# A dilated mixer whose second and third group read a copy of h in class order, written by GpSimd

## The chip, the cores and the metric

The kernel runs on one core of one Trainium2 chip. The metric is the device time of one execution in microseconds. TensorE multiplies (a load of the stationary operand, then the product with the moving operand, into PSUM), VectorE and ScalarE do the elementwise work, GpSimd is nearly unused, and SP's queue issues the loads from memory.

## The reference

Two transformer blocks in sequence on x, 512 tokens of 1024 features: a first block of two layers (an even mixer, a convolutional feed-forward, a dilated mixer, a second convolutional feed-forward) and a second block with modulated layers. Only the dilated mixer matters here. h is the normalised x.

```
z = (h @ w_in).reshape(B, S, 3, 3, 4, 128)      # groups, (q, k, v), heads, features
q = rmsnorm(z[:, :, :, 0], q_gain)
k = rmsnorm(z[:, :, :, 1], k_gain)
v = z[:, :, :, 2]
for g, (window, dilation) in enumerate(((128, 1), (512, 4), (2048, 16))):
    o_g, lse_g = dilated_branch(q[:, :, g], k[:, :, g], v[:, :, g], dilation, window // dilation)
...
wts = softmax(stack(lses), axis=0)
o = sum(wts[..., None] * stack(outs), axis=0)
return o.reshape(B, S, 512) @ w_out
```

A query t of a group attends to t, t - dilation, t - 2 * dilation and so on. So the tokens of groups two and three fall into classes by t modulo the dilation; the kernel uses 4 classes for both (group three masks the keys whose distance within a class is no multiple of 4).

## The kernel before

Features lie on the partitions and tokens on the free axis. h stands in SBUF as 8 k tiles of 128x512, each as a pair of rounded part and rest (`hh`, `hl`); weights come from memory in blocks of 256 columns, as `raw` tiles of 4 k tiles, and are split in units of 2 k tiles into `whi` (ScalarE) and `wlo` (VectorE). Every product is three products (`mm3`: high by high, and two mixed ones). TensorE's order is the order of the program: `gemm` gives feature-major keys and queries, with the weights stationary and 512 columns of h moving into PSUM tile `gm`; `gemm_tok` gives token-major values, with a slice of 128 tokens of h stationary and 256 columns of weights moving into PSUM tile `gt`. After each k tile `tick` issues further splits and the next stages of tasks: `k_norm` and `q_scale` (PSUM tiles `ss` and `qst`, VectorE factors), then `odd_scores` (PSUM tile `os`; VectorE takes the row maximum, ScalarE the exponential into `pr`). A task is issued when a model of the engines' times says that its inputs are there and that PSUM banks are free. `finish(su)` issues all that is left of a list of tasks. SP's loads go out in the order in which a dry run recorded the weights' use, each when a `raw` buffer (there are 4) is free. All 128x512 work tiles come from one pool of 66.

In the dilated mixer, keys and queries of groups one, two and three come first, in this order, with the scores as tasks between them. For groups two and three the ScalarE copies out of PSUM reorder the columns by class (`cls`, `clsps`). Then come the values:

```
for gi in range(3):
    sls = [slice(t * P, (t + 1) * P) for t in range(4)] if gi == 0 else \
          [slice(r, S, 4) for r in range(4)]
    ...
        for t, p in enumerate(self.gemm_tok(w(gi * 6 + 4 + b), NK, h, sls)):
            nc.scalar.activation(vt[t][:, b * 256:(b + 1) * 256], p, AF.Copy)
```

So group one's slices of h are contiguous, those of groups two and three take every fourth token. `finish(su)` stands ahead of group two's values; behind it the tasks `odd_weights` (PSUM tiles `nat` and `cl`) and `odd_turn` (VectorE scales `pr`, TensorE transposes it into `ot`) run between the remaining values. At the end `odd_out` (PSUM tile `opo`) multiplies values and weights.

Of the kernel before, what the change touches and what calls it, by code (L numbers as in the profile page):

```python
# [19 lines left out]
P = 128  # L20
D = 1024
S = 512
# [55 lines left out]
def bcast(ap, off, n):  # L78
    """a row of n elements for every partition"""
    if isinstance(ap, Blank):  # L80
        return ap
    return bass.AP(tensor=ap.tensor, offset=ap.offset + off, ap=[[0, P], [1, n]])


class Blank:
    """stands for any object while the order of the weights is recorded"""
# [11 lines left out]
class Clock:  # L98
    """estimates when the engines get to the instructions, in us, so that they can be issued in a good order"""
# [5 lines left out]
    @staticmethod  # L105
    def span(ap):
        """the tensor's name, and the columns"""
        pitch = ap.ap[0][0]
        a = ap.offset % pitch if pitch else 0
        return ap.tensor.name, a, a + 1 + sum((n - 1) * abs(st) for st, n in ap.ap[1:])  # L110

    def done(self, ap, engine=None):
        """when the data are there, for an engine"""
        name, a, b = self.span(ap)
        return max([f + (0.1 if e != engine else 0.0 if e == "tensor" else 0.05) for c, d, f, e in self.written.get(name, ()) if c < b and a < d], default=0.0)
# [66 lines left out]
class Kern:  # L182
# [82 lines left out]
    def chore(self, gen):  # L265
        """instructions in stages, each issued when its turn has come"""
        c = [gen, False, (), 0.0]
        self.chores.append(c)
        self.step(c)
# [9 lines left out]
    def unit(self, key, k0, n, w, load, hold=False):  # L279
        """n k tiles of weights, split; unless they are held, those before are done with. load: how many  # L280
        k tiles come from memory together with these, if these are the first of them"""
# [24 lines left out]
    def wahead(self):  # L306
        """a split ahead, if the engines have the time"""
# [32 lines left out]
    def weights(self, key, kt, w=256, first=0):  # L340
        """the weights of k tiles first .. first + kt, a k at a time: (k, hi, lo)"""
        for k0, n, (hi, lo) in self.units(key, kt, w, first):
            for k in range(n):
                yield k0 + k, hi[:, k], lo[:, k]

    def passes(self, srcs, kt, ps, done, first=0, tok=False):
        """several passes over the same weights, which stay on chip meanwhile. ps: list of (h, its columns,
        the psum's columns or None for a psum of its own, a function to call before); done(pass, source,
        psums) comes after each source of a pass."""
# [48 lines left out]
    def gemm(self, src, kt, hs, widths=(128, 128), first=0):  # L398
        """hs: list of (list of (hi, lo) per k, N). Returns psum[m][stream]."""
# [11 lines left out]
    def gemm_m(self, src, kt, h, first=0):  # L411
        """the products of 256 columns, a half of the columns after the other: a single psum at a time"""
# [17 lines left out]
    def gemm_tok(self, src, kt, h, sls):  # L430
        """token-major: for each token slice a psum [128, 256]"""
# [10 lines left out]
    def rsqrt_small(self, v, n, y=None):  # L442
        """1/sqrt(v) for a few columns, on DVE."""
# [12 lines left out]
    def square(self, key, x, k):  # L456
        """the running sum of the chunks' squares; until the last chunks two are side by side"""
# [20 lines left out]
    def stream(self, key):  # L478
        """the chunks of a stream: a half of x, or the context"""
        return self.cs if key == "c" else [x[:, HALF[key]] for x in self.x]  # L480

    def begin_norm(self, key):
        """spawns the norm of a stream whose squares are under way, for the next sublayer"""
# [13 lines left out]
    def norm(self, key, xs, hs, G, Sh):  # L497
        """rmsnorm of 256 tokens over the features (partitions and chunks), of sums of squares that are
        under way -> hs, (hi, lo) of each chunk"""
# [53 lines left out]
    def halves(self, off=True):  # L553
        """the passes over the halves of x"""
# [7 lines left out]
    def mid_steps(self, src, res, n=S):  # L562
        """hi and lo of src, into the list res"""
# [11 lines left out]
    # ---- feed-forward: up pairs -> mids -> partial down products into x  # L575
    def ffn(self, up, down, act, gates, after=None, late=None):
        """gates: by stream, "x" and if need be "c" """
# [48 lines left out]
    def final(self, src, mids, gate, first=0, ctx=None, tables="silu_and_others"):  # L626
        """the last products into x, a half of the tokens after the other, each with the start of its norm"""
# [25 lines left out]
    def done(self, mids):  # L653
        """flushes the chores if a mid is still to be issued in part"""
# [3 lines left out]
    def update(self, x, ps, gate, k):  # L658
        """x += gate * ps"""
# [34 lines left out]
    def proj_out(self, src, gate, mids, first=0):  # L694
        """x += gate * W^T mids, over the k tiles from first on"""
# [11 lines left out]
    def firsts(self, srcs):  # L707
        """the first products of a mixer"""
# [8 lines left out]
    # ---- tasks whose instructions go between the k steps of the large products  # L717
# [5 lines left out]
    def step(self, t):  # L723
        """issues the next stage of a task or chore"""
# [11 lines left out]
    def time(self):  # L736
        """where the tensor engine is"""
# [16 lines left out]
    def start(self, t):  # L754
        """when a task can go on: its inputs are there, and its banks free"""
# [36 lines left out]
    def finish(self, ts):  # L792
        """issues all that is left of the tasks; others only where they hold nothing up"""
# [18 lines left out]
    # ---- modulation vectors, a unit of 256 columns at a time  # L812
# [10 lines left out]
    def mod_task(self):  # L823
# [15 lines left out]
        def sums(i, m, r, u0, n):  # L839
            """the sums over the partitions for n units from u0 on"""  # L840
# [42 lines left out]
    # ---- even mixer of the first block  # L883
# [5 lines left out]
    def even_mixer(self):  # L889
# [27 lines left out]
        # linear attention  # L917
# [26 lines left out]
    def k_norm(self, k, res, i, gain, mat, dh, n, perm=None, post=None):  # L944
        """k <- k * rstd * gain, in place"""
# [11 lines left out]
    def rstd_bc(self, sq, n, mat, cnt):  # L957
        """1/sqrt(mean over mat's blocks of sq + eps), replicated over the block's partitions"""
# [15 lines left out]
    def o_norm(self, o, res, i, gain, extra=None, gate=None):  # L974
        """rmsnorm of a head's output over its 128 features, then hi and lo"""
# [13 lines left out]
    def q_scale(self, ps, res, i, gain, mat, nh, dh, perm=None, post=None, front=False):  # L989
        """q with its gain (unnormalised); a task for the row scales rstd / sqrt(dh), token-major [P, 4 * nh]"""  # L990
# [8 lines left out]
        def task():  # L999
# [5 lines left out]
            # (mean + eps) * dh  ->  rsqrt gives rstd / sqrt(dh)  # L1005
# [20 lines left out]
    def softmax(self, s, cc, p, sm, nb):  # L1026
        """p = exp(cc*(s - max)), sm = row sums; nb = -cc*max"""
# [42 lines left out]
    def log_decay(self, ar, gs):  # L1070
        """log decays, token-major (16 times too large), two tiles of [P, 2 * 256]"""
# [17 lines left out]
    def gla(self, gs):  # L1089
# [37 lines left out]
        # attention inside the chunks  # L1127
# [18 lines left out]
        # states  # L1146
        gs["st"] = st = {}
        for c in range(2):
            prev = None
            sts = [self.g("state") for _ in range(2)]  # L1150
            for n0 in (0, 4):
                ns = [n for n in range(n0, n0 + 4) if n < 7]
                # a bank for each row tile of the array
# [35 lines left out]
    # ---- odd mixer of the first block  # L1189
    def odd_mixer(self):  # L1190
# [3 lines left out]
        H = [(h, S)]  # L1194
# [11 lines left out]
        su = []  # L1206
        for gi in range(3):
            kh = []
            if gi == 0:
                pk = self.firsts([w(2), w(3), w(0)])  # L1210
            for b in range(2):
                for m, ps in enumerate(pk[b] if gi == 0 else [p[0] for p in self.gemm(w(gi * 6 + 2 + b), NK, H)]):
                    k = self.g("ok")
                    if gi == 0:
                        nc.scalar.activation(k, ps, AF.Copy)
                    else:
                        nc.scalar.activation(cls(k), clsps(ps), AF.Copy)
                    kh.append(self.spawn(self.k_norm(k, kt, (gi, 2 * b + m), self.v("od_k_gain"), self.ones, 128, S)))
            for b in range(2):
                for m, ps in enumerate(pk[2] if gi == b == 0 else [p[0] for p in self.gemm(w(gi * 6 + b), NK, H)]):  # L1220
                    hd = 2 * b + m
                    qh = self.q_scale(ps if gi == 0 else clsps(ps), qs, (gi, hd), self.v("od_q_gain"),
                                      self.ones[:, 0:1], 1, 128, perm=None if gi == 0 else cls)
                    prob[gi, hd] = [self.g("pr0"), self.g("pr1")] if gi == 0 else [self.g("pr")]
                    su.append(self.spawn(self.odd_scores(gi, hd, kt, qs, prob[gi, hd], sms, nbs), (kh[hd], qh)))
        # values, in the order of the classes
        val = {}
        co = None
        for gi in range(3):
            sls = [slice(t * P, (t + 1) * P) for t in range(4)] if gi == 0 else \  # L1230
                  [slice(r, S, 4) for r in range(4)]
            vt = [self.g("ov") for _ in range(4)]
            for b in range(2):
                if gi == 1 and b == 0:
                    self.finish(su)
                    gs = {}
                    wg = self.spawn(self.odd_weights(lse, sms, nbs, gs))
                    parts = [[] for _ in range(4)]
                    pts = [self.spawn(self.odd_turn(hd, prob, gs, parts[hd]), [wg]) for hd in range(4)]
                    self.wb = 6  # L1240
                for t, p in enumerate(self.gemm_tok(w(gi * 6 + 4 + b), NK, h, sls)):
                    nc.scalar.activation(vt[t][:, b * 256:(b + 1) * 256], p, AF.Copy)
            val[gi] = vt
# [25 lines left out]
    def odd_weights(self, lse, sms, nbs, gs):  # L1269
        """the rows' factors: weight of the group / row sum, [P, 3, (tile, head)]"""  # L1270
# [58 lines left out]
    def odd_turn(self, hd, prob, gs, res):  # L1329
        """the weights of a head, with the rows' factors, transposed"""  # L1330
# [27 lines left out]
    def odd_out(self, hd, parts, val, res):  # L1358
        """sum over the groups of the weighted values of a head"""
# [17 lines left out]
    # ---- attention mixer of the second block  # L1377
# [75 lines left out]
    def attn_unit(self, t, c, qs, kk, va, ao):  # L1453
        """a pair of heads for 128 tokens; keys of the context, then of x"""
# [39 lines left out]
        # the heads' weighted values, side by side on the array, then over the sums  # L1494
# [12 lines left out]
    def stack_q(self, qs, i, res):  # L1507
        """hi and lo of each head of a pair one below the other"""
# [13 lines left out]
    def stack_k(self, ks, i, res, n):  # L1522
        """by head, hi twice and lo twice"""
# [18 lines left out]
    def pool(self, gi, p0, pw, res):  # L1542
        """(window means - p) @ pool_w: the tokens are mixed last, by a banded matrix"""
# [28 lines left out]
    # ---- gated spatial mixer of the second block  # L1572
# [65 lines left out]
    def mods_of(self, key, norm, row):  # L1638
        """the factors and the shift of a norm: (G(k), Sh(k))"""
# [25 lines left out]
    def context(self):  # L1665
        """loads the context and begins its first norm"""
# [63 lines left out]
def lay_out(inputs):  # L1730
    """Layouts of the inputs, and constants of the shapes."""
# [3 lines left out]
    def blocks(w, cols=None):  # L1735
        """[K, M] -> [M/256, 128, K/128, 256]"""
# [5 lines left out]
    def pm(v):  # L1742
        """[.., n*128] -> [128, .. n]"""
# [69 lines left out]
    # by window: the blocks for the first, the inner and the last tokens, then the columns that a neighbour adds to  # L1813
# [34 lines left out]
```

## Time and profile before

| | us |
|---|---|
| three runs | 3411.66, 3412.04, 3418.02 |
| median | 3412.04 |
| span of the profiled execution, first to last instruction | 3414.8 |
| TensorE busy / weight loads busy | 3366.9 / 2939.6 |
| VectorE busy / ScalarE busy / GpSimd busy | 2098.8 / 1252.8 / 5.0 |

The runs are device times. The profiled execution has no time of its own beside its span, which lies inside the three runs. Weight loads overlap products, so the two rows of TensorE are not to be added. All start times below are microseconds from the start of the span; the dilated mixer lies between about 682 and 1010.

### The profile page before, as it was taken

How to read it: one execution, taken by the hardware profiler on the slowest of the kernel's cores; microseconds unless marked ns; L12 is line 12 of the kernel's file. 1: busy time of each engine (PE TensorE's matmuls, PEld its weight loads, DVE VectorE, ACT ScalarE, POOL GpSimd, SP SyncE). 2: the span in 40 equal slices, each digit the busy share in tenths (PEclk: the TensorE clock that was granted, in tenths of full speed). 3: DMA queues.
4: the chain of work that ended last, by engine and by line, in shares of the span. 5: the costliest groups of instructions: out<-in, count | busy, mean ns of one | idle time of the engine just before them, and what ended most of it. 6: DMA issues, size and time to landing. Idle time of an engine off the chain costs nothing.

```text
span 3414.8 us, 48351 instructions
## 1 busy us (share of the span) xinstructions
PE 3366.9 (99%) x19172; PEld 2939.6 (86%) x19172; DVE 2098.8 (61%) x4570; ACT 1252.8 (37%) x2526; POOL 5.0 (0%) x13
## 2 busy tenths in 40 slices
PE   7999999999999999999999998999999999999999
PEld 7688888988998888988888987988898889998888
DVE  5657988767339878864554876755563335463333
ACT  5554434355234334322122356432333233443231
POOL 0000000000000000000000000000000000000000
PEclk9999999999999999999999999999999999999999
DMA  3122444422114444443433321344532223232332
GB/s 111 62 63 81 130 141 125 129 69 81 56 51 124 142 129 130 127 151 100 135 118 111 96 69 38 106 154 145 155 112 88 95 93 106 91 93 93 99 97 71
DMA packets 105845, 355.73 MB, mean 104 GB/s; under 512 B 12673, under 2 KB 18962, under 8 KB 105618
## 3 DMA queue, kind: packets, MB, share of 16 engines
q1 hardware_dynamic: 105618, 352.64, 33.3%
q8 instruction: 150, 2.46, 0.3%
q14 instruction: 77, 0.63, 0.1%
HBM read 350.50 MB, written 2.10 MB: 103 GB/s over the span
## 4 chain that ended last, share of the span: by engine, by line
PE 91%; DVE 5%; ACT 3%; issue 1%; DMA 0%; SPq 0%; DVEq 0%; ACTq 0%
PE gm L172 80%; PE gt L172 5%; ACT ap L172 1%; PE ds L172 1%; DVE wlo L172 1%; DVE nt L172 1%; PE ss L172 1%; PE os L172 1%; DVE amx L172 0%; PE oa L172 0%; ACT L172 0%; DVE hl L172 0%; PE opo L172 0%; DVE x L172 0%; PE qst L172 0%
## 5 line engine op out<-in xcount | busy, mean ns | idle before, releaser
L172 PE MATMUL gm<-hh,whi 128*128 128x512 f32 (+1 forms) x3000 | 1095.1, 365 | 5.0 <-ACT hh L172 4.2
L172 PE MATMUL gm<-hl,whi 128*128 128x512 f32 (+1 forms) x3000 | 1084.8, 362 | 1.2 <-DVE hl L172 1.2
L172 PE MATMUL gm<-hh,wlo 128*128 128x512 f32 (+1 forms) x3000 | 1082.4, 361 | 3.5 <-DVE wlo L172 3.4
L172 DVE TENSOR_TENSOR wlo<-raw,whi 128x512 fp32r<-128x512 f32 (+1 forms) x1028 | 661.0, 680 | 113.5 <-ACT whi L172 113.2
L172 ACT ACTIVATE whi<-raw 128x512 fp32r<-128x512 f32 (+1 forms) x1028 | 581.5, 616 | 293.8 <-DMA raw<-in_ffn_w_dram 115.2
L172 PEld LDWEIGHTS gm<-hh,wlo 128*128 128x128 f32 x3000 | 568.1, 189 | 93.0 <-DVE wlo L172 4.2
L172 PEld LDWEIGHTS gm<-hh,whi 128*128 128x128 f32 x3000 | 569.1, 190 | 79.2 <-ACT hh L172 4.4
L172 PEld LDWEIGHTS gm<-hl,whi 128*128 128x128 f32 x3000 | 569.0, 190 | 73.4 <-issue 2.5
L172 PE MATMUL gm<-mh,whi 128*128 128x512 f32 (+1 forms) x1696 | 577.2, 340 | 0.0
L172 PE MATMUL gm<-ml,whi 128*128 128x512 f32 (+1 forms) x1696 | 573.4, 338 | 1.1 <-DVE ml L172 1.1
L172 PE MATMUL gm<-mh,wlo 128*128 128x512 f32 (+1 forms) x1696 | 572.1, 337 | 0.0
L172 DVE TENSOR_TENSOR ga<-ga,gm 128x512 f32<-128x512 f32 (+1 forms) x110 | 68.0, 633 | 498.2 <-PE gm L172 329.0
L172 PEld LDWEIGHTS gm<-mh,wlo 128*128 128x128 f32 x1696 | 322.1, 190 | 34.9
L172 PEld LDWEIGHTS gm<-ml,whi 128*128 128x128 f32 x1696 | 322.3, 190 | 29.2 <-DVE ml L172 1.6
L172 PEld LDWEIGHTS gm<-mh,whi 128*128 128x128 f32 x1696 | 322.2, 190 | 29.0 <-issue 0.9
L172 ACT ACTIVATE ga<-gm 128x512 f32<-128x512 f32 (+1 forms) x110 | 58.8, 554 | 716.0 <-PE gm L172 716.0
L172 DVE SCALAR_TENSOR_TENSOR macc<-rawm,sc,macc 128x256 f32<-128x256 f32 x504 | 243.8, 484 | 15.4
L172 DVE SCALAR_TENSOR_TENSOR x<-gm,modt,x 128x256 f32<-128x256 f32 (+1 forms) x184 | 105.8, 607 | 226.6 <-PE gm L172 226.5
L172 PEld LDWEIGHTS gm<-hc,whi 128*128 128x128 f32 x736 | 135.9, 190 | 29.0 <-ACT whi L172 1.5
L172 DVE SCALAR_TENSOR_TENSOR cy<-gm,vec,cy 128x511 f32<-128x511 f32 (+1 forms) x176 | 127.7, 746 | 47.9 <-ACT cy L172 44.7
L172 PE MATMUL gt<-whi,hh 128*128 128x256 f32 x448 | 146.8, 328 | 1.2 <-DVE qv L172 0.7
L172 PE MATMUL gm<-hc,whi 128*128 128x256 f32 x736 | 146.1, 282 | 1.3 <-ACT whi L172 1.3
(286 smaller groups left out, 3271.4 us busy)
## 6 DMA issues: line engine op xcount, KB each, us to landing
raw<-in_ffn_w_dram SPq DMA_DIRECT2D x256, 512.0 KB, 4.4
rawm<-in_w_mod_dram SPq DMA_DIRECT2D x144, 512.0 KB, 4.3
raw<-in_ffn_w_up_dram SPq DMA_DIRECT2D x88, 512.0 KB, 3.8
raw<-in_ffn_w_down_dram SPq DMA_DIRECT2D x40, 512.0 KB, 3.7
raw<-in_od_w_in_dram SPq DMA_DIRECT2D x36, 512.0 KB, 3.8
raw<-in_ev_w_in_dram SPq DMA_DIRECT2D x24, 512.0 KB, 4.1
raw<-in_w_in_c_dram SPq DMA_DIRECT2D x16, 512.0 KB, 4.5
raw<-in_w_in_a_dram SPq DMA_DIRECT2D x10, 512.0 KB, 4.3
```

The costliest lines, as they stand in the source:

```text
L172: return f(*args, **kwargs)
```

## The change

h is copied once, after group one's queries, into 16 new work tiles (`ph`, `pl`), with the columns in the order of the classes. The 16 copies are GpSimd instructions; each reads every fourth column and writes contiguous columns. Keys, queries and values of groups two and three read this copy (`hp`) in place of h. Their ScalarE copies out of PSUM, for keys and queries, no longer reorder, and all values take contiguous slices of 128 columns. The values of group one move from behind all queries to a place between group one's queries and group two's keys. `finish(su)` and the start of `odd_weights` move behind the first block of group two's values; three blocks of values follow them. The number of products stays the same. Elsewhere the diff only empties comments and docstrings.

```diff
-        H = [(h, S)]
...
-        su = []
+        su, val = [], {}
+        hp = []
+
+        def values(gi, b, hh):
+            if b == 0:
+                val[gi] = [self.g("ov") for _ in range(4)]
+            sls = [slice(t * P, (t + 1) * P) for t in range(4)]
+            for t, p in enumerate(self.gemm_tok(w(gi * 6 + 4 + b), NK, hh, sls)):
+                nc.scalar.activation(val[gi][t][:, b * 256:(b + 1) * 256], p, AF.Copy)
+
         for gi in range(3):
             kh = []
             if gi == 0:
                 pk = self.firsts([w(2), w(3), w(0)])
+            H = [(hp if gi else h, S)]
             for b in range(2):
                 for m, ps in enumerate(pk[b] if gi == 0 else [p[0] for p in self.gemm(w(gi * 6 + 2 + b), NK, H)]):
                     k = self.g("ok")
-                    if gi == 0:
-                        nc.scalar.activation(k, ps, AF.Copy)
-                    else:
-                        nc.scalar.activation(cls(k), clsps(ps), AF.Copy)
+                    nc.scalar.activation(k, ps, AF.Copy)
...
-                    qh = self.q_scale(ps if gi == 0 else clsps(ps), qs, (gi, hd), self.v("od_q_gain"),
-                                      self.ones[:, 0:1], 1, 128, perm=None if gi == 0 else cls)
+                    qh = self.q_scale(ps, qs, (gi, hd), self.v("od_q_gain"), self.ones[:, 0:1], 1, 128)
...
-        # values, in the order of the classes
-        val = {}
-        co = None
-        for gi in range(3):
-            sls = [slice(t * P, (t + 1) * P) for t in range(4)] if gi == 0 else \
-                  [slice(r, S, 4) for r in range(4)]
-            vt = [self.g("ov") for _ in range(4)]
-            for b in range(2):
-                if gi == 1 and b == 0:
-                    self.finish(su)
-                    gs = {}
-                    wg = self.spawn(self.odd_weights(lse, sms, nbs, gs))
-                    parts = [[] for _ in range(4)]
-                    pts = [self.spawn(self.odd_turn(hd, prob, gs, parts[hd]), [wg]) for hd in range(4)]
-                    self.wb = 6
-                for t, p in enumerate(self.gemm_tok(w(gi * 6 + 4 + b), NK, h, sls)):
-                    nc.scalar.activation(vt[t][:, b * 256:(b + 1) * 256], p, AF.Copy)
-            val[gi] = vt
+            if gi == 0:
+
+                for xs in h:
+                    hp.append((self.h("ph"), self.h("pl")))
+                    for x, y in zip(xs, hp[-1]):
+                        nc.gpsimd.tensor_copy(cls(y), clsps(x))
+                for b in range(2):
+                    values(0, b, h)
+
+        values(1, 0, hp)
+        self.finish(su)
+        gs = {}
+        wg = self.spawn(self.odd_weights(lse, sms, nbs, gs))
+        parts = [[] for _ in range(4)]
+        pts = [self.spawn(self.odd_turn(hd, prob, gs, parts[hd]), [wg]) for hd in range(4)]
+        self.wb = 6
+        values(1, 1, hp)
+        for b in range(2):
+            values(2, b, hp)
```

## Rows read from the trace of the kernel before

**Rows 1.** The page's head: span, busy time, share of the span, instructions.

```profile
span 3414.8 us, 48351 instructions
...
PE 3366.9 (99%) x19172; PEld 2939.6 (86%) x19172; DVE 2098.8 (61%) x4570; ACT 1252.8 (37%) x2526; POOL 5.0 (0%) x13
```

**Rows 2.** The chain that ended last, by engine, share of the span.

```profile
PE 91%; DVE 5%; ACT 3%; issue 1%; DMA 0%; SPq 0%; DVEq 0%; ACTq 0%
```

**Rows 3.** Stretches of the mixer: busy us of each engine, granted clock, DMA.

```profile
720.00:740.00 20.00, 20.00 (x99) 15.58 (x98) 16.83 (x41) 8.90 (x16) 0.00 (x0) 1.00 0.00 1
740.00:760.00 20.00, 20.00 (x110) 16.15 (x110) 13.64 (x60) 12.05 (x37) 0.00 (x0) 1.00 0.06 16
...
900.00:920.00 20.00, 20.00 (x99) 20.00 (x99) 12.16 (x56) 3.21 (x8) 0.00 (x0) 0.86 0.17 53
```

**Rows 4.** Tile gt, 852 to 873, group one: ns min/median/max, first and last start.

```profile
L172 PEld LDWEIGHTS gt<-wlo,hh x45: 188/192/192, 852.2 to 872.9; 128*128 128x128 f32 x45
L172 PE MATMUL gt<-wlo,hh x44: 280/283/287, 852.3 to 872.0; 128*128 128x256 f32 x44
```

**Rows 5.** Tile gt, 923 to 980, groups two and three.

```profile
L172 PE MATMUL gt<-wlo,hh x75: 393/395/403, 923.0 to 979.9; 128*128 128x256 f32 x75
L172 PEld LDWEIGHTS gt<-whi,hl x74: 329/330/333, 923.1 to 979.3; 128*128 128x128 f32 x74
```

**Rows 6.** The chain in order of time, 640 to 1050: start, us, engine, tile, instructions.

```profile
772.73 10.92 PE gm L172 x48
...
863.37 2.93 PE gt L172 x24
...
894.59 1.69 PE nat L172 x16
...
904.83 1.69 PE cl L172 x16
...
949.73 30.81 PE gt L172 x132
```

**Rows 7.** Tile ok: the key copies out of PSUM, all three groups.

```profile
L172 ACT ACTIVATE ok<-gm x12: 581/596/600, 709.5 to 824.6; 128x512 f32<-128x512 f32 x12
```

**Rows 8.** GpSimd's instructions by shape: busy us, mean ns, idle time ahead of them.

```profile
L172 POOL MEMSET att<- 128x512 f32 x4 | 2.1, 530 | 195.3 <-PE gm L172 192.5 <-ACT eb L172 2.7
L172 POOL CAST bf_mb<-cst 128x128 bf16<-128x128 f32 x1 | 0.8, 775 | 0.0
...
L172 POOL CAST bf_ident<-cst 128x128 bf16<-128x128 f32 x1 | 0.5, 458 | 7.6 <-DMA cst<-in_cst_dram 7.6
...
L1844 POOL MEMSET const-float32-1.0<- 128x1 f32 x1 | 0.1, 100 | 0.0
```

**Rows 9.** ScalarE in order of time: the query copies, then group two's first keys.

```profile
732.64 0.60 ACT L172 ACTIVATE qsq<-gm 128x512 f32<-128x512 f32 x1 [5.47 <-PE gm L172]
...
734.18 0.70 ACT L172 ACTIVATE q<-gm,vec 128x512 f32<-128x512 f32 x1
...
754.50 1.07 ACT L172 ACTIVATE ok<-gm 128x512 f32<-128x512 f32 x2
```

**Rows 10.** GpSimd in order of time, the kernel's start.

```profile
21.59 0.67 POOL L172 CAST bf_mc<-cst 128x128 bf16<-128x128 f32 x1 [13.14 <-DMA cst<-in_cst_dram]
```

**Rows 11.** VectorE in order of time, the same microseconds.

```profile
21.42 1.41 DVE L172 TENSOR_TENSOR nsq<-nsq 128x512 f32<-128x512 f32 x2
```

**Rows 12.** Tile nsq: the additions of squares in the whole kernel.

```profile
L172 DVE TENSOR_TENSOR nsq<-nsq x110: 415/426/694, 5.2 to 3050.1; 128x256 f32<-128x256 f32 x66, 128x512 f32<-128x512 f32 x44
```

**Rows 13.** SP's own waits, 680 to 1000: us in total, times, longest.

```profile
SPq L172 <- DVE wlo L172: 282.2, 34, 46.9
...
SPq L172 <- DMA raw<-in_od_w_in_dram: 1.4, 1, 1.4
```

**Rows 14.** Tile os, 850 to 880: the last scores of group three.

```profile
L172 PE MATMUL os<-ok,q x24: 271/274/328, 849.8 to 875.9; 128*128 128x128 f32 x24
...
L172 ACT ACTIVATE pr<-os,nbs,cc x13: 452/457/461, 850.5 to 876.8; 128x128 f32<-128x128 f32 x13
```

**Rows 15.** VectorE in order of time: the scalings of all four heads.

```profile
907.81 10.29 DVE L172 TENSOR_SCALAR pr<-pr,co 128x128 f32<-128x128 f32 x48
```

## The prediction

> **What bounds the kernel now.** I read the page's totals first, then the chain of waits, then the dilated mixer alone. TensorE is busy for 3366.9 of 3414.8 us [rows 1], and the chain that ended last lies on it for 91% [rows 2]. So the time is the sum of TensorE's work, and an edit counts only if it shortens that work or makes TensorE wait. In stretches of 20 us inside the mixer TensorE is busy for the whole 20 us, VectorE for 13.64 to 16.83 in the part with the scores and 12.16 in the part with the values, GpSimd never [rows 3]. What differs is the weight load: 15.58 and 16.15 us of it with keys and queries, but all 20.00 with the values of groups two and three. A busy TensorE is therefore not TensorE at its best, and the next view asks what one product costs there.
>
> The products for the values take slices of h as the stationary operand. In group one the slice is contiguous: loading 128x128 takes 192 ns and the product behind it 283 [rows 4]. In groups two and three the slice takes every fourth token: the same load takes 329 to 330 ns and the product 395, with operands of the same shape and type [rows 5]. The pitch, which is what the chain pays, comes from pure pieces of it: 24 contiguous products in 2.93 us are 0.1221 us each, 132 strided ones in 30.81 us are 0.2334 [rows 6].
>
> **The change part by part.** *Strided loads become contiguous.* A block of values is 8 k tiles by 4 token slices by 3 products, 96 products; groups two and three have 4 blocks, 384 products. All of them now read a contiguous slice of the copy: 384 x (0.2334 - 0.1221) = 42.7 us less on TensorE. In one window here the granted clock is 0.86, a mean over time at full and at half clock [rows 3]; I credit nothing for it, since the 0.2334 was read behind it.
>
> *Keys and queries of groups two and three.* They still have 512 moving columns and the same number of products. The ScalarE copies out of PSUM lose their strided read, but the twelve key copies, four contiguous and eight strided, all took 581 to 600 ns [rows 7]. Nothing.
>
> *Sixteen GpSimd copies, 128x512, each reading every fourth column.* No such copy is in the trace. Below: the 128x512 memset, 0.53 us, which reads nothing. Above: the slowest 128-column cast, 0.775, times four, 3.10. The nearest row is the cast that ran alone, 0.458; less the 0.10 of a one-column memset, times four, plus 0.10, it gives 1.53 us, which I take [rows 8]. Sixteen make 24.5 us (8.5 to 49.6). GpSimd has no other work here, so nothing is queued behind them; who waits is the first key product of group two. The copies stand in the program behind the last query copy of group one, which ends at 734.9 [rows 9]; if the engine gets there no earlier, they end at 759.4. When are they needed? Group one's last query product is done at 732.6. Then come the moved values: 192 x 0.1221 = 23.4 us. Group one's scores run among them: from 732.64 to 754.50 TensorE did one block of keys, 10.9 us [rows 6], and other work, mostly these scores, for the other 11.0 [rows 9]. So group two's keys start near 732.6 + 23.4 + 11.0 = 767.0 and take a k tile every 6 x 0.2275 = 1.37 us, the last at 776.6. The values that are moved ahead are the cover; without them group two's first block of keys, which ended at 754.5, would want the last copy by then, and 759.4 - 754.5 = 4.9 us would show. At 1.53 us I cost the copies at nothing on TensorE; they are late from 41.7 / 16 = 2.6 us each.
>
> *What the copies do to VectorE.* Two GpSimd casts, from 21.59 on, ran beside 128x512 VectorE additions of two SBUF operands; two of these took 1.41 us [rows 10, 11], and none of the 110 in the kernel is longer than 694 ns [rows 12]. The casts took 0.67 and 0.775 instead of the 0.458 of the one that ran alone [rows 8, 10]. So the trace shows GpSimd yielding, not VectorE. I take 1 us, with bounds 0 and the 15 us of the first rival. The Trainium skill ("SBUF — State Buffer", section "SBUF: two separate sides") speaks against the change here: VectorE and GpSimd share a pair of ports as an exclusive lock, and a VectorE instruction with two SBUF inputs blocks fully while a GpSimd instruction that reads SBUF holds it. By that the sum would be that of the first rival; the additions beside the casts do not show it, though casts of 128 columns hold anything only briefly.
>
> *Values of group one move ahead of group two.* The step carries 192 products, 8 PSUM copies on ScalarE, 8 splits of weights (one instruction each on ScalarE and VectorE) and 4 loads of 512 KB on SP's queue; the order of the weights is recorded anew, so splits and loads move with it. SP waited for VectorE's splits to free its buffers (282.2 us in 34 waits) and for a transfer of this stage 1.4 us [rows 13]: buffers pace it, not transfers. A contiguous block of values wants 1 MB in 96 x 0.1221 = 11.7 us, what keys want in 10.9. Nothing.
>
> *Work tiles.* Counted from the code, about 44 of the 66 are held when group one's queries are done (16 of h, 18 of split weights, 4 keys, 4 queries, 2 squares). The copy adds 16 and the early values 4: 64, until h goes free at the end of group one's values. A split can then wait for a tile that TensorE is still reading, one k step of 12 products, 1.5 us, mostly covered by the weights already split. I take 0.5, bounds 0 and 3.
>
> *The forced end of the scores comes earlier.* `finish(su)` stood behind two blocks of group one's values and found nothing left; now one block lies between the last query and it. From the last query products at 852.3, 96 products of values reach to about 866, while the last score ran at 875.9 [rows 14]. Some five scores are left, each 0.3 us of TensorE and 0.65 of ScalarE (457 ns and its accumulator's read). Bounds: nothing, if the free banks take them, and 10 us if every one of those lies open. Nearest is ScalarE's 5 x 0.65 = 3.3 us less TensorE's own 1.5; I take 1.5.
>
> *The weights of the groups behind it.* They have three blocks as cover, 288 products, not four. Before, the chain used 384 - 132 = 252 of them until its last transposition (the 132 behind it stand in one piece) [rows 6]. The waits in it are shorter than their new cover: between `nat` and `cl` lie 36 products, 4.4 us. VectorE's 48 scalings, 10.29 us [rows 15], run ahead of transpositions that are spread over eight steps. Nothing.
>
> Sum: 42.7 - 1.0 - 0.5 - 1.5 = 39.7 us. The profiled span is 3414.8, 2.8 above the median and inside the runs, so I subtract from the median: 3412.0 - 39.7 = 3372.3.
>
> **The rivals.** *GpSimd holds VectorE up.* If each copy blocks VectorE for its length, 24.5 us are lost there, of which 40 - 16.83 - 13.64 = 9.5 us of idle time between 720 and 760 [rows 3] take the first part; 15 us reach TensorE through the scores that wait for VectorE's factors. Time: 3387. Against it the row of the additions; for it the key norms, whose steps have two SBUF operands.
>
> *The copies come late.* At 3.10 us each they end at 784.5, 7.9 us behind the last k tile's need: 3380. Against it: 3.10 scales a cast that lay beside VectorE's additions, and GpSimd may start before 734.9, since it waits for no query.
>
> *The scores lie open.* The full 10 us at `finish(su)` instead of 1.5: 3381.
>
> *Slower.* One mechanism reaches it: copies so slow that group two's keys stand still for longer than is gained. Break-even is at (41.7 + 39.7) / 16 = 5.1 us a copy; at 6 us the lateness is 54.3 and the time 3427. That is nearly twice the upper bound.
>
> *No effect.* The slow loads could come from the stretch, not from the stride. Against it: the slow rows begin with the first strided slice and nothing else changes.
>
> **How the numbers follow.** Chances: forecast 0.66, VectorE held up 0.12, copies late 0.10, scores open 0.06, slower 0.03, no effect 0.03. The likeliest case alone runs from 3368 to 3378. The range takes in the first three rivals: high 3388; low 3366, which is 3412.0 - 42.7 = 3369.3 with no losses, less the 3 us that the runs' own spread may hide. A change under 0.2%, 6.8 us, can't be told from none here: faster 0.94, same 0.03, slower 0.03.
>
> **What would show it.** Right: strided loads gone, every product of values at a pitch near 0.122; the values of groups two and three, 384 products, in some 47 us; sixteen GpSimd copies of about 1.5 us that end before group two's first key; TensorE without waits there, and at most a gap of a few us behind the first block of group two's values. Wrong: copies over 2.6 us with TensorE waiting for GpSimd; VectorE instructions of two SBUF operands twice as long beside a copy and scores that wait for them; or loads of the copy that still take 330 ns.

## The result, and the profile after

The changed kernel takes 3386.2 us, the median of four runs (3384.2 to 3387.9), against 3414.8 for the kernel before, the median of four. The ratio is 0.9913, 95% interval 0.9901 to 0.9926: about 29 us faster, not 40. That lies inside the range, outside the likeliest case's own 3368 to 3378, and within a microsecond of the first rival, 3387.

To see where the time went, one stretch is nearly free of the runs' spread (two traces of the changed kernel, from two chips, give 259.3 and 259.0 us for it). It begins with a piece of 234 products early in the mixer, 29.39 us long in every kernel, and ends at the first product of `odd_out`. The chain in order of time (start, us, tile, count), of the kernel before:

```profile
691.31 29.39 PE gm L172 x234
...
980.54 13.40 PE opo L172 x120
```

and after the change:

```profile
689.38 29.39 PE gm L172 x234
...
948.72 13.40 PE opo L172 x120
```

The stretch is 980.54 - 691.31 = 289.2 us before and 948.72 - 689.38 = 259.3 after, 29.9 less: all of the gain lies there. I call it the mixer stretch below.

The page's head, which answers to [rows 1]:

```profile
span 3384.7 us, 48370 instructions
...
PE 3327.9 (98%) x19172; PEld 2898.5 (86%) x19172; DVE 2113.2 (62%) x4570; ACT 1251.6 (37%) x2526; POOL 28.0 (1%) x29
```

TensorE and its loads lost about 40 us each, but the span only 30. VectorE, with the same 4570 instructions, gained 14 us, and that is the trail. First the part that went as forecast, tile gt from 880 to 960, against [rows 5]:

```profile
L172 PEld LDWEIGHTS gt<-wlo,ph x128: 187/192/192, 887.1 to 947.8; 128*128 128x128 f32 x128
L172 PE MATMUL gt<-wlo,ph x128: 274/283/283, 887.2 to 947.9; 128*128 128x256 f32 x128
```

The values' loads take 192 ns and their products 283, like group one's in [rows 4]. In the chain 96 of them follow each other in 11.57 us, 0.1205 each. At `finish(su)`, behind the first of the four blocks, the chain runs for some 1.1 us over VectorE and ScalarE (the kernel before has such a piece of the same length at 866.62); TensorE stands idle for only 0.2 us of the 20 from 900 on:

```profile
901.49 0.30 DVE mx L172
...
902.07 0.56 ACT pr L172 x2
...
904.05 11.57 PE gt L172 x96
```

What was given back lies earlier. The windows, against [rows 3] (busy us of TensorE, its loads, VectorE, ScalarE and GpSimd, then the granted clock):

```profile
720.00:740.00 20.00, 19.76 (x122) 16.88 (x120) 19.19 (x17) 6.96 (x13) 15.22 (x11) 1.00 0.00 1
740.00:760.00 20.00, 11.91 (x68) 11.08 (x68) 17.09 (x61) 2.03 (x7) 7.73 (x6) 0.76 0.00 0
760.00:780.00 20.00, 19.80 (x138) 18.26 (x139) 8.93 (x26) 10.31 (x33) 0.00 (x0) 0.90 0.17 53
```

TensorE is idle for 8.1 of the 20 us from 740 on, and the clock, mixed of full and half speed, is 0.76 and then 0.90; before, it had no idle time there and a clock of 1.00. From 720 to 740 VectorE is busy for 19.19 us and finishes 17 instructions, where [rows 3] have 41 in 16.83. TensorE's waits of the mixer name what was late:

```profile
PE os L172 <- DVE qv L172: 5.0, 1, 5.0
PE gt L172 <- ACT pr L172: 3.5, 2, 2.1
```

The products behind the waits are slow as well. In the chain 18 of the values' products, behind a wait for `pr`, take 4.12 us, 0.229 each, and 12 soon after them 1.49 us, 0.124 each; the granted clock is 0.57 from 757 to 765 and 1.00 from 765 to 770:

```profile
760.20 4.12 PE gt L172 x18
...
765.46 1.49 PE gt L172 x12
```

GpSimd and VectorE in order of time show why. GpSimd's copies:

```profile
724.78 1.16 POOL L172 CAST ph<-hh 128x512 fp32r<-128x512 f32 x1 [507.07 <-PE gm L172]
725.88 1.55 POOL L172 CAST pl<-hl 128x512 fp32r<-128x512 f32 x1
727.39 1.57 POOL L172 CAST ph<-hh 128x512 fp32r<-128x512 f32 x1
...
745.56 1.10 POOL L172 CAST ph<-hh 128x512 fp32r<-128x512 f32 x1
746.61 1.12 POOL L172 CAST pl<-hl 128x512 fp32r<-128x512 f32 x1
```

VectorE beside them:

```profile
724.29 0.69 DVE L172 SCALAR_TENSOR_TENSOR rb<-ksq,rb 128x512 f32<-128x512 f32 x1
725.02 1.47 DVE L172 SCALAR_TENSOR_TENSOR ok<-ok,vec,rb 128x512 f32<-128x512 f32 x1
726.42 1.57 DVE L172 TENSOR_TENSOR ksq<-rb 128x512 f32<-128x512 f32 x1
...
743.21 1.46 DVE L172 SCALAR_TENSOR_TENSOR ok<-ok,vec,rb 128x512 f32<-128x512 f32 x1
744.59 0.15 DVE L172 TENSOR_SCALAR qv<-qst 128x4 f32<-128x4 f32 x1
...
746.72 1.03 DVE L172 SCALAR_TENSOR_TENSOR rs_t<-cc 128x4 f32<-128x4 f32 x1
...
748.18 0.16 DVE L172 SCALAR_TENSOR_TENSOR rs_t<-cc 128x4 f32<-128x4 f32 x1
...
756.00 0.28 DVE L172 TENSOR_REDUCE mx<-os 128x1 f32<-128x128 f32 x1
```

With the first copy the key norm's steps go from 0.69 to about 1.5 us, and copies and steps come one for one: starts of copies at 725.88 and 727.39, ends of steps between them. Even a step on 4 columns, 0.16 us alone, takes 1.03 beside a copy. A copy without a large neighbour takes 1.10 to 1.16. So the two engines take turns. A copy and a step together begin anew every 1.51 us, where copies alone follow each other in 1.05 us and steps alone in 0.73: all but 0.27 us of a pair lies one behind the other. The first maximum of a score is at 756.00; before, with this stretch beginning 1.93 us later, it was at 745.15:

```profile
745.15 0.28 DVE L172 TENSOR_REDUCE mx<-os 128x1 f32<-128x128 f32 x1
```

VectorE is 12.8 us late.

### The profile page after: what moved, and what is told of

It is laid out like the page before. It is cut to its first block, busy times and chain, and to the rows that moved or that the text cites. A ratio compares the mean times of both kernels' runs of the same rounds, so it can differ in the third digit from the quotient of the medians.

```text
span 3384.7 us, 48370 instructions
## 1 busy us (share of the span) xinstructions
PE 3327.9 (98%) x19172; PEld 2898.5 (86%) x19172; DVE 2113.2 (62%) x4570; ACT 1251.6 (37%) x2526; POOL 28.0 (1%) x29
## 4 chain that ended last, share of the span: by engine, by line
PE 89%; DVE 6%; ACT 3%; issue 1%; DMA 1%; SPq 0%; DVEq 0%; ACTq 0%
PE gm L172 81%; PE gt L172 4%; ACT ap L172 1%; PE ds L172 1%; DVE wlo L172 1%; PE ss L172 1%; DVE nt L172 1%; PE oa L172 1%; DVE amx L172 0%; DVE rs_t L172 0%; PE os L172 0%; ACT L172 0%; DVE ksq L172 0%; DVE x L172 0%; PE opo L172 0%
## 5 line engine op out<-in xcount | busy, mean ns | idle before, releaser
L172 PE MATMUL gm<-hh,whi 128*128 128x512 f32 (+1 forms) x2872 | 1041.0, 362 | 4.9 <-ACT hh L172 4.1
L172 PE MATMUL gm<-hl,whi 128*128 128x512 f32 (+1 forms) x2872 | 1034.5, 360 | 1.2 <-DVE hl L172 1.2
L172 PE MATMUL gm<-hh,wlo 128*128 128x512 f32 (+1 forms) x2872 | 1031.9, 359 | 3.5 <-DVE wlo L172 3.4
L172 PEld LDWEIGHTS gm<-hh,wlo 128*128 128x128 f32 x2872 | 543.9, 189 | 87.1 <-DVE wlo L172 4.2
L172 PEld LDWEIGHTS gm<-hh,whi 128*128 128x128 f32 x2872 | 544.7, 190 | 73.5 <-ACT hh L172 4.4
L172 PEld LDWEIGHTS gm<-hl,whi 128*128 128x128 f32 x2872 | 544.7, 190 | 68.4 <-DVE hl L172 1.8
L172 ACT ACTIVATE nsq<-x 128x256 f32<-128x256 f32 x160 | 60.8, 416 | 179.4 <-DVE x L172 175.9
```

What stands on the lines that cost most here:

```text
L172: return f(*args, **kwargs)
```

## The experiments

Theory A: GpSimd's copies hold up VectorE, TensorE waits for its factors, and half clock follows the waits. Theory B: the moved values and the tight work tiles delay the stage, whoever copies. Theory C: contiguous loads are worth less than 42.7 us. Each run is read by its time and by the mixer stretch.

**ScalarE makes the copies.**

```diff
-                        nc.gpsimd.tensor_copy(cls(y), clsps(x))
+                        nc.scalar.activation(cls(y), clsps(x), AF.Copy)
```

> The sixteen copies of h are made by ScalarE, at the same place, instead of GpSimd; nothing else changes. Theory A (each GpSimd copy holds up VectorE's instructions with SBUF operands; TensorE then waits for group one's query factors, and its granted clock falls behind the waits; 13.4 us in all between group one's keys and group three's last query): the key norm's steps are back at 0.68 to 0.75 us, no wait of TensorE for qv, and about 3386.2 - 13.4 = 3373 us; ScalarE's copies, some 0.6 us each and 9.6 us together, fall into the stretch from about 735 to 745 in which it was idle. Theory B (the moved values and the 64 held work tiles delay the stage, whoever copies): 3384 to 3388. Theory C (contiguous weight loads are worth only some 29 us): 3384 to 3388 as well.

3378.2 us, ratio 0.9894 (0.9878 to 0.9911), mixer stretch 938.80 - 687.01 = 251.8:

```profile
687.01 29.39 PE gm L172 x234
...
938.80 13.40 PE opo L172 x120
```

VectorE, and TensorE's longest wait:

```profile
721.20 0.69 DVE L172 TENSOR_TENSOR ksq<-ksq,hv 128x512 f32<-128x512 f32 x1
```

```profile
PE gt L172 <- ACT pr L172: 3.9, 2, 2.6
```

The steps are back at 0.69 and the wait for `qv` is gone, as A says; B and C, 3384 or more, are out as whole causes. But 5 us more remained than A expected, behind a wait for ScalarE:

```profile
730.43 1.18 ACT L172 ACTIVATE ph<-hh 128x512 fp32r<-128x512 f32 x1
731.46 1.20 ACT L172 ACTIVATE pl<-hl 128x512 fp32r<-128x512 f32 x1
...
745.89 1.13 ACT L172 ACTIVATE pl<-hl 128x512 fp32r<-128x512 f32 x1
746.89 0.48 ACT L172 ACTIVATE pr<-os,nbs,cc 128x128 f32<-128x128 f32 x1
```

My 0.6 us for a ScalarE copy was wrong: with every fourth column read from SBUF it takes 1.18, a pitch of 1.03, 16.5 us in all. The exponentials stand behind them in ScalarE's order, the first right behind the last copy, and the values waited 3.9 us for them; that they waited for the PSUM banks which the scores held is read from the program.

**Contiguous loads alone**, in the kernel before; the values of groups two and three stand in the wrong token order.

```diff
-            sls = [slice(t * P, (t + 1) * P) for t in range(4)] if gi == 0 else \
-                  [slice(r, S, 4) for r in range(4)]
+            sls = [slice(t * P, (t + 1) * P) for t in range(4)]
```

> The kernel before, with contiguous slices of 128 tokens of h for the values of all three groups, so that the values of groups two and three stand in the wrong token order; no copies, no moved values. It prices the contiguous loads alone. Theories A and B: 384 x (0.2334 - 0.1221) = 42.7 us less than before, about 3372 us. Theory C: about 3386 us, some of the gain being eaten by waits in the shorter stretch (for the weights of the groups, for splits or for PSUM).

3369.8 us, the median of two runs, ratio 0.9867 (0.9847 to 0.9887):

```profile
687.26 29.39 PE gm L172 x234
...
932.64 13.40 PE opo L172 x120
```

245.4 us, 43.8 less than before. Theory C falls; the forecast's gross term of 42.7 holds. And the slow loads come from the stride, not from the stretch: nothing else was changed here, and the loads take 192 ns.

**Copies alone**, in the kernel before, into tiles that nobody reads.

```diff
+            if gi == 0:
+                for xs in h:
+                    for x in xs:
+                        nc.gpsimd.tensor_copy(cls(self.h("ph")), clsps(x))
```

> The kernel before, with the sixteen GpSimd copies of h added behind group one's queries, into tiles that nobody reads. Theory A: VectorE's key norm steps take about 1.5 us each instead of 0.7, TensorE waits for group one's factors, and the time rises by 8 to 14 us, to 3423 to 3429. Theories B and C: no change, 3412 to 3418.

3425.4 us, ratio 1.0031 (1.0016 to 1.0047), and TensorE waits:

```profile
PE os L172 <- DVE qv L172: 6.6, 4, 2.6
```

```profile
689.88 29.39 PE gm L172 x234
...
991.43 13.40 PE opo L172 x120
```

301.6 us, 12.3 more than before. No values were moved and nothing reads the copies: GpSimd's copies cost this by themselves, as A said.

**Copies that read consecutive columns**, so that groups two and three mix the wrong tokens.

```diff
-                        nc.gpsimd.tensor_copy(cls(y), clsps(x))
+                        nc.gpsimd.tensor_copy(y, x)
```

> The kernel after the change, but each GpSimd copy reads consecutive columns instead of every fourth, so that the copy has the columns in their natural order and groups two and three mix the wrong tokens. It tells what the stride of the copies costs. Theory A: the uncontended copy falls from 1.10 us to between 0.53 (a memset of this shape) and 0.9; VectorE is held up for less, and the time falls by 3 to 8 us, to 3378 to 3383. Theories B and C: 3386 us whatever a copy takes.

3375.7 us, the median of two runs, ratio 0.9885 (0.9865 to 0.9904), 2 us below the least that I expected:

```profile
685.30 29.39 PE gm L172 x234
...
936.76 13.40 PE opo L172 x120
```

The mixer stretch is 251.5. A copy beside a step, one alone, and a key norm step beside a copy:

```profile
733.53 1.07 POOL L172 CAST pl<-hl 128x512 fp32r<-128x512 f32 x1
734.55 0.61 POOL L172 CAST ph<-hh 128x512 fp32r<-128x512 f32 x1
```

```profile
722.98 0.98 DVE L172 TENSOR_TENSOR ksq<-ksq,hv 128x512 f32<-128x512 f32 x1
```

Alone, a copy falls from 1.10 to 0.61 us, and VectorE's step from 1.5 to 0.98: what VectorE loses per step falls from about 0.8 to 0.3 us, and the loss in the stretch, counted from 245.9 (next run), from 13.4 to 5.6. Copy and step begin anew every 1.02 us. Length of the copy sets the price, as A says. But waits of the values for `pr`, 3.5 us, remained here too, which raised a theory B2: the move has a price of its own, in banks.

**The move without copies**; groups two and three read h itself and mix the wrong tokens.

```diff
-                    hp.append((self.h("ph"), self.h("pl")))
-                    for x, y in zip(xs, hp[-1]):
-                        nc.gpsimd.tensor_copy(cls(y), clsps(x))
+                    hp.append(xs)
```

> The kernel after the change without the copies: groups two and three read contiguous slices of h itself, so that they mix the wrong tokens. The values of group one stay at their new place. It prices the move alone. Theory B2 (the move has a price of its own: the second block of group one's values needs four PSUM banks that group one's first scores still hold, since VectorE works through the factors of all four heads first): two waits of the values for ScalarE's pr remain, 2 to 4 us with some us of half clock behind them, and the time is 3374 to 3377, about 5 us above the contiguous slices at the old place (3369.8). Theory A alone (only the copies cost something): 3369 to 3371 and no such waits.

3371.6 us, ratio 0.9869 (0.9853 to 0.9886):

```profile
688.40 29.39 PE gm L172 x234
...
934.33 13.40 PE opo L172 x120
```

245.9 us, 0.5 above the contiguous loads at the old place, and of the waits for `pr` one of 0.2 us is left. B2 falls: these waits appear only when VectorE or ScalarE is late with group one's scores. The move costs half a microsecond, so the copies, with the 16 tiles that they fill, cost 259.3 - 245.9 = 13.4 us of the mixer stretch.

**Late copies.** In the kernel before, the GpSimd copies go behind group three's queries; keys and queries read h as before, group one's values keep their place, and from there on six units of weights are held ahead.

```diff
+        hp = []
+        self.wb = 6
+        for xs in h:
+            hp.append((self.h("ph"), self.h("pl")))
+            for x, y in zip(xs, hp[-1]):
+                nc.gpsimd.tensor_copy(cls(y), clsps(x))
...
-                for t, p in enumerate(self.gemm_tok(w(gi * 6 + 4 + b), NK, h, sls)):
+                for t, p in enumerate(self.gemm_tok(w(gi * 6 + 4 + b), NK, hp if gi else h, sls)):
```

(with contiguous slices `sls` for all groups)

> Keys and queries of all groups and the values of group one as in the kernel before, the sixteen GpSimd copies behind the last query of group three, and the values of groups two and three from the copy; the weights held ahead are cut to six units from there on. Theories A and B2: VectorE has no key norms left there, only 8 splits and the factors of two heads with two SBUF operands, so the copies delay little; they take 16 x 1.5 = 24 us at most, beside group one's values (23.4 us and some scores); no values among group one's scores, so no wait for banks. About 3414 - 44.5 + 2 = 3372 us, with up to 4 us more if the last copies come late for the first values of group two. If the copies cost the same 8 us and more wherever they stand: 3378 or above.

3374.9 us, ratio 0.9879 (0.9864 to 0.9894), mixer stretch 249.3:

```profile
688.13 29.39 PE gm L172 x234
...
937.44 13.40 PE opo L172 x120
```

Group one's values stand at their old place here, so the run to compare with is the contiguous loads alone, 245.4: the same sixteen copies, beside fewer VectorE steps on SBUF, cost 3.9 us instead of 13.4, where I expected 2. VectorE there:

```profile
840.19 1.00 DVE L172 TENSOR_TENSOR rs_t<-rs_t,qv 128x4 f32<-128x4 f32 x1
...
850.39 0.94 DVE L172 TENSOR_TENSOR wlo<-raw,whi 128x512 fp32r<-128x512 f32 x1 [0.24 <-ACT whi L172]
851.25 0.28 DVE L172 TENSOR_REDUCE mx<-os 128x1 f32<-128x128 f32 x1
851.57 0.21 DVE L172 TENSOR_SCALAR nbs<-mx,cc 128x1 f32<-128x1 f32 x1
```

GpSimd copied from 850.73 to 853.8 in this run, so the maximum, which reads PSUM, and the one-column step behind it were not held up at all.

**Mixed late copies**: GpSimd copies the high parts, ScalarE the low ones, one at a time between the products.

```diff
-            for x, y in zip(xs, hp[-1]):
-                nc.gpsimd.tensor_copy(cls(y), clsps(x))
+            nc.gpsimd.tensor_copy(cls(hp[-1][0]), clsps(xs[0]))
+
+        def low():
+            for xs, ys in zip(h, hp):
+                nc.scalar.activation(cls(ys[1]), clsps(xs[1]), AF.Copy)
+                yield
+        self.chore(low())
```

> As the late copies, but GpSimd copies only the eight high parts, and ScalarE the eight low parts, one at a time between the products. Theories A and B2: GpSimd is done in 12 us, ScalarE's copies take 1.04 us each in a stretch where it is 40% busy; 3370 to 3373 us, at or below the late copies by GpSimd alone. If ScalarE's copies hold up the last scores: 3374 to 3377.

3374.4 us, the middle of four runs between 3368.7 and 3374.9, ratio 0.9875 (0.9860 to 0.9890):

```profile
690.10 29.39 PE gm L172 x234
...
936.58 13.40 PE opo L172 x120
```

246.5 us, 1.1 above the contiguous loads alone. The time itself was above the expected 3370 to 3373, and can't be told from the late copies' 3374.9. So the kernel was run again, beside the changed kernel on one chip:

> The mixed late copies once more, beside the kernel after the change on the same chip. Between the first products of the mixer and the first product of odd_out it took 246.5 us, against 259.3 after the change and 289.2 before. If that stretch is all that differs: about 42.7 us less than before, 12.8 us less than after the change.

> The kernel after the change, unaltered, on the same chip as the mixed late copies: 28 to 30 us less than before, and 12.8 us more than the mixed late copies.

3372.4 us (3370.3 to 3374.4), ratio 0.9873 (0.9860 to 0.9887), against 3386.2 and 0.9915 (0.9901 to 0.9928) for the changed kernel: 13.8 us better, as the stretches said. The mixer stretch is 246.5 in this trace too. Of the versions that leave nothing out it is the best here by the stretch, 246.5 against 249.3 for the late copies; that lead over the late copies does not show in their times.

## Why the prediction was right, and where it was wrong

*The range and the time.* The range held because it takes in the first rival, which had a chance of 0.12; the likeliest case, 3368 to 3378 at 0.66, did not come. That 3386.2 lies so near the rival's 3387 is partly luck. Its working differs from what happened (below), and the forecast subtracted from a median of three runs, 3412.0, where the four runs beside the result have 3414.8. Also, with its 15 us in place of the 1 us of the forecast's sum, the rival comes to 3386.3 and not to 3387.

*The gross term.* 42.7 us forecast, 43.8 in the stretch with contiguous loads alone. Right, and with it the reading that a busy TensorE hid a slow weight load.

*Sixteen copies of 1.53 us.* Right in length, 1.455 us on average for the high parts and 1.515 for the low ones, and they were not late: the last ended at 747.7, group two's keys began at 778.7. But the agreement was partly luck: alone a copy takes 1.10, the rest is waiting for VectorE. And they began at 724.78, not at the 734.9 that the forecast worked with, and so fell on group one's key norms.

*What the copies do to VectorE.* This step failed. I took 1 us; the runs show 13.4. The reason I gave, that the additions beside the casts in [rows 10 to 12] were not longer, was true of 128-column casts and did not carry over to 512 columns. The first rival, which let every copy block VectorE, is what happened, but not by its working of 24.5 us of blocking less 9.5 us of idle time. Each copy sets VectorE's next step back by 1.51 - 0.73 = 0.78 us, which makes 12.5 us for sixteen; VectorE came 12.8 us late, and no idle time took any of it up. TensorE waited 5.0 + 3.5 = 8.5 us for it. The rest is half clock behind the waits, for which neither the forecast nor the rival had a term: in the 40 us from 740 on, the granted clock of 0.76 and 0.90 means about 13.6 us at 1.2 instead of 2.4 GHz. Product by product, 47 of group one's values there stand 0.213 us apart instead of 0.120, which is 4.4 us, and the first score takes 0.67 instead of 0.25. Waits and slow products together are 13.3 of the 13.4 us.

The Trainium skill ("SBUF — State Buffer", section "SBUF: two separate sides") has this rule: VectorE instructions with two SBUF inputs, or in a mode that takes both ports, and GpSimd instructions that read SBUF lock each other out, whole instructions at a time. These traces agree: 0.69 against about 1.5 us beside a 1.10 us copy, 0.98 beside a 0.61 us one, and 0.28 unchanged for a maximum read from PSUM. Only the 0.27 us by which a pair is shorter than its two parts is not in the rule. I gave it 0.12; I had weighed it against too small an instruction.

*Moved values, work tiles, `finish(su)`.* 2.0 us together in the forecast. The move without copies measured 0.5 for the moved values and `finish(su)`. The 16 more work tiles are not in that run; their 0.5 us was not measured by itself, but among TensorE's waits in the changed kernel's mixer there is none for split weights. The three blocks behind `finish(su)` were cover enough, as argued.

So the sum should have read 43.8 - 0.5 - 13.4 = 29.9 us. That it gives what the mixer stretch shows is no test, since the three are differences along one chain of runs, from the kernel before to the changed one. The test is the copies alone, outside this chain: 12.3 us.

## What to carry to other kernels

An instruction moved to an idle engine is not free if a neighbour's instructions on SBUF have to take turns with it, as VectorE's did here with GpSimd's: look at what the neighbour runs in those microseconds, and put the copy where the neighbour reads PSUM or rests. Price such a meeting from rows of the same length; here a 128-column cast lay beside a 512-column addition and the addition showed nothing. And when a lag reaches TensorE, add the slower clock behind the wait: here it made a third of the loss, 4.8 of 13.4 us.

## What the runs showed of the hardware

A read of every fourth fp32 column from SBUF is slow on three engines: TensorE's weight load 330 instead of 192 ns, GpSimd's copy 1.10 instead of 0.61 us, ScalarE's copy 1.18 us where its split, another instruction of the same shape that reads consecutive columns, takes 0.62. ScalarE's read from PSUM at the same step costs nothing [rows 7].
